# A hybrid decoder layer: in-projection tiles by Strassen's method first, and all heads' keys ahead of the delta rules

## The chip, the core and the metric

The kernel runs on one core of a Trainium2 chip. A core has TensorE (PE, matrix products into PSUM banks; PEld are its weight loads), VectorE (DVE), ScalarE (ACT), GpSimd (POOL) and SyncE (SP). Each works through a queue of its own in order; they wait for one another by semaphores. DMAs are issued here from SP's and POOL's queues. The metric is device time of one execution in microseconds (us), the median of several runs; lower is better.

## The reference

One layer of a decoder, over 512 prompt tokens and 8 sample tokens (520 columns, NTOK), in float32:

```python
xn   = rmsnorm(h, norm_mix)                         # 2048 wide
proj = xn @ w_in                                    # 2048 -> 5136: q | k | v | z | beta, decay | pool
q,k,v = silu(short_conv(proj[q,k,v], conv_w))       # causal, 4 taps; 8 heads of 128 each
q,k  = l2norm(q) * 128**-0.5, l2norm(k)
o    = gated_delta_chunked(q, k, v, g, beta)        # prompt; sample tokens: one recurrent step
dn   = rmsnorm(o, dn_norm) * silu(z)
pool = multiscale_pool(proj[pool])                  # 4 groups, trailing means of 2, 4, 8, 16
h    = h + concat(dn, pool) @ w_out
h    = h + (silu(gate) * up) @ w_down               # SwiGLU, d_ff = 5632
y    = rmsnorm(h, norm_final)
```

The delta rule of a head needs, for each block of tokens, the inverse of a unit lower triangular matrix 1 + M with M = strict(beta k k' decay).

## The kernel before, in words

Every float32 operand is cut into two fp32r halves: `hi`, a cast on ACT, and `lo`, the rest, by a subtraction on DVE. A product takes three passes, hi·hi, hi·lo and lo·hi. Activations lie transposed: `xh`, `xl` are the halves of the normed x as 16 tiles of 128 x 520 (token columns). A weight tile of 128 columns comes by SP as two `raw` loads of 512 KB, each cut once.

`product()` makes one 128-column tile of the projection: 16 k x 3 passes x 2 chunks of columns (264 and 256) = 96 matmuls into two banks named `mm`. The second chunk follows the first by SKEW = 3 k's. When a chunk is done, an eviction (`normed_out`, L259, DVE) scales it out of its bank. After each k, `weave.step()` lets other work, written as generators that yield, put its instructions into the queues; `weave.add(gen, queue, n)` starts one after n such steps. One product is 16 steps. So what stands between the matmuls of a product on PE is set by these counts.

A Strassen pair (`Pair`, `strassen()`; the out-projection, gate/up and down stages use them already) makes two 128-column tiles at once from half matrices: 7 products of 8 k x 3 passes with 260 columns, 168 matmuls into banks named `dn` in place of 192. It needs sums of weight blocks (DVE, `add`), sums of the activations' quarters (the forms T1 to T4) and sums of the results (`combine`, `out`).

The in-projection's order before: the transposes of x and the tiles k0, k1 in a first phase; then, for b in 0, 1 (four heads each): four k tiles, with `keys(h)` woven under them 16 steps apart; `eliminate(b)`; four z tiles; four times the q and the v tile of a head and, woven under the next, its `delta(h)`. Behind come the sample tokens' rules, woven under 8 pool tiles.

- `qkv_tile` evicts a tile to `ext` and applies the convolution on DVE (L739, L741: four operations of 128x512) and SiLU on ACT.
- `keys(h)` needs kT: it makes k k' and k's transpose on PE, norms, then `nn` (L783 on DVE, in mixb, one slot for each head of four) and `kd`. The four 32 x 32 diagonal blocks of nn go to DRAM (`nd_d`, four SP DMAs) and are then zeroed by four POOL memsets, which wait for those DMAs.
- `eliminate(b)` loads the diagonal blocks of four heads as `nb`, 64 partitions, and inverts them by 31 pairs of dependent DVE operations (L809 tm, L811 u). u and its transposed copy `ut` (L814) go to DRAM (`ud_d`); `qv_tiles` reads a head's blocks back as `utf`, four DMAs.
- `delta(h)` begins on PE with nn x utf (L833), then solves between blocks and runs the recurrence over four chunks.

Of the kernel before, what the change touches and what calls it, by code (L numbers as in the profile page):

```python
# [69 lines left out]
def decoder_kernel(ctx, tc, x_prompt, x_sample, state_delta, state_conv, state_pool, norm_mix, w_in,  # L70
# [94 lines left out]
    def step(acc, w, hi, lo, ci, k):  # L165
        c0, c1 = CHUNKS[ci]
        wh, wl = w[k]
        te.matmul(acc[ci], wh, hi[k][:, c0:c1], start=(k == 0), stop=False)  # L168
        te.matmul(acc[ci], wh, lo[k][:, c0:c1], start=False, stop=False)  # L169
        te.matmul(acc[ci], wl, hi[k][:, c0:c1], start=False, stop=(k == len(w) - 1))  # L170

    def product(w, hi, lo, evict, skew=SKEW):
# [8 lines left out]
        for i in range(K + skew):  # L181
            if i < K:
                step(acc, w, hi, lo, 0, i)
                if i == K - 1:
                    finish(0)
            if i >= skew:
                step(acc, w, hi, lo, 1, i - skew)
                if i < K + skew - 1:
                    weave.step()
# [71 lines left out]
    def columns():  # L261
        ext = pre.tile([P, 3 + SEQ], F32, tag="ext", name="ext", bufs=2)
        pool.memset(ext[:, 0:3], 0.0)
        return ext

    def to_columns(ext, t, ci, acc):
        if ci == 0:
            normed_out(ext[:, 3:3 + 256], acc, NB, 264, 0)
            normed_out(ccs[:, :, t], acc, 0, NB, 0)
        else:  # L270
            normed_out(ext[:, 3 + 256:3 + 512], acc, 264, NTOK, 264)

    with tc.tile_pool(name="ph0", bufs=2) as ph0, tc.high_priority(offset=10 * AHEAD), tc.manual_schedule():
        pr0 = ph0.tile([KT, P], F32, name="pr0", bufs=1)
        pr1 = ph0.tile([112, P], F32, name="pr1", bufs=1)
        pr2 = ph0.tile([32, P], F32, name="pr2", bufs=1)  # L280
        wba_raw = ph0.tile([P, KT, 16], F32, name="wba_raw", bufs=1)
        ss0 = ph0.tile([P, 10], F32, name="ss0", bufs=1)
        rs0 = ph0.tile([P, 8], F32, name="rs0", bufs=1)
        sel = ph0.tile([P, NB], F32, name="sel", bufs=1)
        xts = [ph0.tile([P, D if ti else P], F32, name=f"xt{ti}", bufs=1) for ti in range(5)]

        def span(ti):
            return slice(NB + P * (ti - 1), NB + P * ti) if ti else slice(0, NB)

        def square_sums(ti, eng, cols=slice(0, D), j=0):  # L290

            src, out = xts[ti][:, cols], ss0[:, 2 * ti + j:2 * ti + j + 1]
            sq = ph0.tile([P, D // 2], mybir.dt.bfloat16, name=f"sq{j}", bufs=1)[:, :src.shape[1]]
            if eng is act:
                act.activation(sq, src, AF.Square, accum_out=out)
            else:
                dve.scalar_tensor_tensor(sq, src, 1.0, src, op0=ALU.mult, op1=ALU.mult, accum_out=out)

        def roots(ti):
            s, r = ss0[:, 2 * ti:2 * ti + 1], rs0[:, ti:ti + 1]  # L300
            dve.tensor_tensor(s, s, ss0[:, 2 * ti + 1:2 * ti + 2], op=ALU.add)
            dve.tensor_scalar(s, s, 1.0 / D, EPS, op0=ALU.mult, op1=ALU.add)
            pow_mhalf(r, s)

        def diagonal(ti):
            dg = ph0.tile([P, P], F32, name="dg")
            dve.tensor_scalar(dg, ident, rs0[:, ti:ti + 1], None, op0=ALU.mult)
            return dg

        def spread(dg):  # L310
            pb = pst()
# [100 lines left out]
        for i in range(4):  # L412
            B[i].turn((0,))

# [1664 lines left out]
```

## Time and profile before

| | us |
|---|---|
| median of three runs | 2162.64 (2162.12 to 2162.88) |
| profiled execution | 2162.58 |
| its span | 2160.9 |
| PE busy in it | 2134.7 |
| DVE busy | 1746.6 |
| ACT busy | 928.6 |
| mean granted clock of TensorE | 0.999 |

The profile is of one execution; the span goes from its first instruction to its last. Busy time counts an instruction from start to end, and matmuls overlap, so that the spacing of their starts, not their duration, tells what one costs. A row of a group reads: line, engine, operation, output<-input, sizes, x count, busy us, mean ns, and the idle time before with what ended it. A row of the timeline reads: start, duration, engine (SPq is SP's queue of DMAs), line, operation, and in brackets the idle time before it and its releaser.

### The profile page before, as it was taken

To read this page: it belongs to the slowest core of one execution; us is meant where nothing else is said; L and a number is where in the kernel's file an instruction comes from. 1 tells how busy PE (TensorE), PEld (TensorE's weight loads), DVE (VectorE), ACT (ScalarE), POOL (GpSimd) and SP (SyncE) were. 2 spreads that over 40 slices of the span, in tenths; PEclk is the share of its full clock that TensorE was granted. 3 is DMA by queue.
4 is the path that set the end of the run, shared out by engine and by line. 5 is a ranking of instruction groups with operands and counts; after the bars stand their busy time and mean duration, and the time that the engine had idled before them with its cause. 6 is when DMAs were issued, how large, how long until landed. Compare 5 with 4: busy or idle time off the path is not lost.

```text
span 2160.9 us, 42982 instructions
## 1 busy us (share of the span) xinstructions
PE 2134.7 (99%) x17809; PEld 2127.9 (98%) x17809; DVE 1746.6 (81%) x2620; ACT 928.6 (43%) x1402; POOL 432.9 (20%) x512
## 2 busy tenths in 40 slices
PE   7999999999999999999999999999999999999998
PEld 7999999999999999999999999999999999999998
DVE  7686667666499979988888888988877898887997
ACT  5533443433264545434434434434434444435444
POOL 2210110101012212233233233232113302003100
PEclk9999999999999999999999999999999999999999
DMA  8343234323445443554554554554456746438333
GB/s 271 93 115 88 78 97 111 89 76 87 124 126 161 147 124 108 157 162 142 148 163 137 151 165 141 146 162 137 122 147 187 235 111 205 115 103 251 89 108 119
DMA packets 442498, 297.06 MB, mean 137 GB/s; under 512 B 26556, under 2 KB 423253, under 8 KB 438957
## 3 DMA queue, kind: packets, MB, share of 16 engines
q1 hardware_dynamic: 422877, 220.01, 36.2%
q0 software_dynamic: 18256, 73.55, 10.7%
q8 instruction: 140, 2.29, 0.5%
q10 hardware_dynamic: 1168, 0.74, 0.1%
q14 instruction: 57, 0.47, 0.1%
HBM read 251.47 MB, written 43.43 MB: 136 GB/s over the span
## 4 chain that ended last, share of the span: by engine, by line
PE 88%; DVE 7%; ACT 2%; issue 1%; DMA 1%; POOL 1%; SPq 0%; DVEq 0%; ACTq 0%; POOLq 0%
PE dn L1225 21%; PE dn L1224 21%; PE dn L1226 21%; PE mm L168 6%; PE mm L170 6%; PE mm L169 6%; DVE lo L1218 1%; PE dn L852 1%; DVE lo L137 1%; DMA st<-a_d 1%; DVE raw L1246 0%; POOL st L1778 0%; PE dn L962 0%; PE dn L859 0%; DVE tm L809 0%
## 5 line engine op out<-in xcount | busy, mean ns | idle before, releaser
L1217 ACT CAST hi<-raw 128x1024 fp32r<-128x1024 f32 (+1 forms) x422 | 427.5, 1027 | 404.2 <-DVE raw L1246 202.1
L1218 DVE TENSOR_TENSOR lo<-raw,hi 128x1024 fp32r<-128x1024 f32 (+1 forms) x422 | 529.2, 1275 | 88.0 <-ACT hi L1217 86.1
L168 PE MATMUL mm<-xh,hi 128*128 128x256 f32 (+1 forms) x1280 | 379.6, 297 | 2.6 <-DVE mixa L259 2.6
L170 PE MATMUL mm<-xh,lo 128*128 128x256 f32 (+1 forms) x1280 | 361.8, 283 | 1.5 <-DVE lo L137 1.5
L169 PE MATMUL mm<-xl,hi 128*128 128x256 f32 (+1 forms) x1280 | 361.4, 282 | 1.3 <-DVE xl L350 1.1
L168 PEld LDWEIGHTS mm<-xh,hi 128*128 128x128 f32 x1280 | 241.4, 189 | 3.7 <-DVE mixa L259 3.2
L169 PEld LDWEIGHTS mm<-xl,hi 128*128 128x128 f32 x1280 | 241.7, 189 | 1.9 <-DVE xl L350 1.9
L170 PEld LDWEIGHTS mm<-xh,lo 128*128 128x128 f32 x1280 | 240.8, 188 | 1.7 <-DVE lo L137 1.7
L1225 PE MATMUL dn<-b21l,hi 128*128 128x260 f32 x620 | 175.7, 283 | 0.3 <-DVE b21l L1788 0.3
L1226 PE MATMUL dn<-b21h,lo 128*128 128x260 f32 x620 | 175.4, 283 | 0.0
L1246 DVE TENSOR_TENSOR raw<-raw 128x1024 f32<-128x1024 f32 (+1 forms) x130 | 173.5, 1335 | 2.2
L1224 PE MATMUL dn<-b21h,hi 128*128 128x260 f32 x620 | 174.9, 282 | 0.0
L1226 PE MATMUL dn<-b11h,lo 128*128 128x260 f32 x612 | 173.2, 283 | 1.2 <-DVE lo L1218 1.2
L1225 PE MATMUL dn<-b11l,hi 128*128 128x260 f32 x612 | 173.3, 283 | 0.0
L1224 PE MATMUL dn<-b11h,hi 128*128 128x260 f32 x612 | 172.7, 282 | 0.0
L1224 PE MATMUL dn<-T1h,hi 128*128 128x260 f32 x556 | 158.1, 284 | 0.0
L1225 PE MATMUL dn<-T1l,hi 128*128 128x260 f32 x556 | 157.7, 284 | 0.0
L1226 PE MATMUL dn<-T1h,lo 128*128 128x260 f32 x556 | 156.7, 282 | 0.0
L1224 PE MATMUL dn<-B22h,hi 128*128 128x260 f32 x548 | 155.9, 284 | 0.0
L1225 PE MATMUL dn<-B22l,hi 128*128 128x260 f32 x548 | 155.6, 284 | 0.0
L1226 PE MATMUL dn<-B22h,lo 128*128 128x260 f32 x548 | 154.6, 282 | 0.4 <-DVE lo L1218 0.4
L135 ACT CAST hi<-raw 128x1024 fp32r<-128x1024 f32 (+2 forms) x86 | 87.1, 1014 | 150.5 <-PE mm L169 146.2
(659 smaller groups left out, 6420.8 us busy)
## 6 DMA issues: line engine op xcount, KB each, us to landing
raw<-in_w_gate_up_dram SPq DMA_DIRECT2D x134, 512.0 KB
raw<-in_w_in_dram SPq DMA_DIRECT2D x79, 512.0 KB
a_d<-mixa POOLq DMA_DIRECT2D x22, 1040.0 KB, 5.5
raw<-in_w_down_dram SPq DMA_DIRECT2D x48, 448.0 KB
mixb<-in_w_gate_up_dram SPq DMA_DIRECT2D x41, 512.0 KB
raw<-in_w_out_dram SPq DMA_DIRECT2D x25, 512.0 KB
st<-a_d POOLq DMA_DIRECT2D x49, 260.0 KB, 6.4
raw<-in_w_down_dram SPq DMA_DIRECT2D x24, 512.0 KB
```

The lines of the kernel that those rows point to most:

```text
L135: act.copy(hi[:, r], raw[:, r])
L137: dve.tensor_tensor(lo[:, r], raw[:, r], hi[:, r].bitcast(F32), op=ALU.subtract)
L168: te.matmul(acc[ci], wh, hi[k][:, c0:c1], start=(k == 0), stop=False)
L169: te.matmul(acc[ci], wh, lo[k][:, c0:c1], start=False, stop=False)
L170: te.matmul(acc[ci], wl, hi[k][:, c0:c1], start=False, stop=(k == len(w) - 1))
L852: te.matmul(yp[0:96, c, j], xt_[:, c, :], udf[:, c, j] if it == 0 else v3(cur)[:, c, j], start=True, stop=True)
L1217: act.copy(hi, raw)
L1218: dve.tensor_tensor(lo, raw, hi.bitcast(F32), op=ALU.subtract)
L1224: te.matmul(acc, wh[:, k, :], xf[:, k, :], start=start and k == 0, stop=False)
L1225: te.matmul(acc, wh[:, k, :], xg[:, k, :], start=False, stop=False)
L1226: te.matmul(acc, wl[:, k, :], xf[:, k, :], start=False, stop=stop and k == wh.shape[1] - 1)
L1246: dve.tensor_tensor(r[name], r[a], r[b], op=op)
```

## The change

- The in-projection begins with five pairs of tiles, k2 to k7 and z0 to z3: (k2, k3) and (k4, k5) as plain pairs in the same half matrices (192 matmuls of 260 columns), while ACT and DVE make the forms from x in mixa and mixb, then (k6, k7), (z0, z1), (z2, z3) by Strassen. T1 takes the place of a quarter of xh, xl; at the last pair that quarter is made again from x in DRAM (`xs_d`), under the next product, which therefore begins with its second eight k's.
- Every q, k, v tile is evicted whole and goes through DRAM (`c_d`, a POOL DMA); `convolved()` reads it back and does convolution and SiLU when it is wanted.
- `keys(h)` of all eight heads follow one another, five steps between nn and the next part, under q and v products. Heads 4 to 7 keep kT in mixa[4..6], nn in mixa[7] alone and kd in one buffer, and store all three to DRAM (`kept_d`); `come_back(h)` fetches them when head h-4 is done.
- One `eliminate()` works on all heads, 128 partitions. It reads back utf of heads 0 and 1 and adds `delta(0)`, 60 steps later; each delta adds the next.
- The products that follow: q0, v0, q1, v1, ... q6, v6, z4, z5, q7, v7, z6, z7, then the pool tiles.

The helpers of the Strassen pairs move up in the text unchanged and are left out here, as is the making of the forms.

```diff
+    class InPair(Pair):
+        def __init__(self, t0):
+            self.out_tiles = {}
+            super().__init__(lambda i, j: win_view(in_cols(t0 + i))[:, 8 * j:8 * j + 8, :], self.to)
+            self.t0 = t0
+        def to(self, i, half, a, b):
...
+            dve.tensor_tensor(o[:, c], a, b, op=ALU.add)
+            dve.tensor_tensor(o[:, c], o[:, c], rb[:, c], op=ALU.mult)
+            if t >= 24:
+                act.activation(o[:, c], o[:, c], AF.Silu)
+            elif not first:
+                stored(o, t)
...
+        plain_pairs = InPair(10), InPair(12)
+        pairs = [InPair(14), InPair(24), InPair(26)]
...
+        plain_pairs[0].plain(to_plain)
+        plain_pairs[1].plain(to_strassen)
...
+            if j == 0:
+                pool.dma_start(b12, xs_d[0:8].rearrange("k p c -> p k c")[:, :, HALF:])
...
+                for k in range(8):
+                    act.activation(hi[:, k, :], b12[:, k, :], AF.Copy, scale=nmix(k))
+                for k in range(8):
+                    dve.scalar_tensor_tensor(lo[:, k, :], b12[:, k, :], nmix(k), hi[:, k, :].bitcast(F32),
+                                             op0=ALU.mult, op1=ALU.subtract)
+        strassen(pairs, fb[:, 0:HG * P], after, xap)
...
+    def stored(o, t):
+        pool.tensor_copy(ccs[:, :, t], o[:, 0:NB])
+        pool.tensor_copy(ccp[:, :, t], o[:, NTOK - 3:NTOK])
+        pool.dma_start(c_d[t], o[:, NB:NTOK])
...
+        def convolved(x, t):
+            pool.memset(x[:, 0:3], 0.0)
+            sp.dma_start(x[:, 3:3 + SEQ], c_d[t])
+            y = d1tile("y", [P, SEQ], "y")
...
+        def places(h):
+            a, b = (mixb[:, h, :], mixb[:, 4 + h, :]) if h < 4 else (mixa[:, 4 + (h - 4) % 3, :], mixa[:, 7, :])
+            return a[:, NB - 3:NTOK], b[:, 0:SEQ]
+        def come_back(h):
+            kd = kds[h] = d1tile("kd", [P, SEQ], "kd")
+            for i, x in enumerate((mixb[:, h % 4, NB:NTOK], mixb[:, 4 + h % 4, 0:SEQ], kd)):
+                sp.dma_start(x, kept_d[h - 4, i])
...
         def keys(h):
-            kT, nn = mixb[:, h % 4, 0:SEQ], mixb[:, 4 + h % 4, 0:SEQ]
-            kd = kds[h] = d1tile("kd", [P, SEQ], "kd")
+            x, nn = places(h)
+            kT = x[:, 3:3 + SEQ]
+            kd = kds[h] = d1tile("kd" if h < 4 else "qts", [P, SEQ], "kd")
+            if h + 2 < H:
+                take_k(h + 2)
...
-            yield 6 if h < 3 else 2
+            yield 5
...
+            if h >= 4:
+                for i, y in enumerate((kT, nn, kd)):
+                    sp.dma_start(kept_d[h - 4, i], y)
+            if h == H - 1:
+                weave.add(eliminate(), 1)
...
-        def eliminate(b):
-            nb = d1tile("nb", [64, 32, 32], "nb")
+        def eliminate():
+            nb = d1tile("nb", [P, 32, 32], "nb")
...
+            for h in range(2):
+                load_u(h)
+            take_qv(0)
+            weave.add(delta(0), 0, 60)
             yield 1
...
-        for b in range(2):
-            for h in range(4 * b, 4 * b + 4):
-                qkv_tile(1, h, mixb[:, h % 4, 0:SEQ],
-                         {0: ext_first, 1: ext_second}.get(h))
...
-                weave.add(keys(h), 1, 16)
-            weave.add(eliminate(b), 1)
-            for h in range(4 * b, 4 * b + 4):
-                z_tile(h)
-            for h in range(4 * b, 4 * b + 4):
-                qv_tiles(h)
+        for h in range(2):
+            take_k(h)
+        weave.add(states())
+        weave.add(gates(), 1)
+        for h in range(H):
+            weave.add(keys(h), 1)
+        for h in range(H):
+            qkv_tile(h, None if h else w_next)
+            qkv_tile(16 + h)
+            for z in {6: (4, 5), 7: (6, 7)}.get(h, ()):
+                z_tile(z)
```

What this does to the queues shows at three places.

DVE, the end of the elimination. Before, in `eliminate(0)` (tm is the product with a column of nb, u the running inverse, ut its transposed copy, lo a weight cut, ext an evicted tile):

```order
L809 TENSOR_TENSOR tm<-nb,u 64x87
L811 TENSOR_TENSOR u<-u,tm 64x3x29
L809 TENSOR_TENSOR tm<-nb,u 64x60
L811 TENSOR_TENSOR u<-u,tm 64x2x30
L809 TENSOR_TENSOR tm<-nb,u 64x31
L811 TENSOR_TENSOR u<-u,tm 64x31
L814 COPY ut<-u 64x1024
L137 TENSOR_TENSOR lo<-raw,hi 128x1024
L259 TENSOR_TENSOR ext<-mm,rb 128x256
```

After:

```order
L261 TENSOR_TENSOR ext<-mm,rb 128x264
L1202 TENSOR_TENSOR u<-u,tm 128x6x26
L1200 TENSOR_TENSOR tm<-nb,u 128x135
L1202 TENSOR_TENSOR u<-u,tm 128x5x27
L1200 TENSOR_TENSOR tm<-nb,u 128x112
L1202 TENSOR_TENSOR u<-u,tm 128x4x28
L1200 TENSOR_TENSOR tm<-nb,u 128x87
L1202 TENSOR_TENSOR u<-u,tm 128x3x29
L1200 TENSOR_TENSOR tm<-nb,u 128x60
L1202 TENSOR_TENSOR u<-u,tm 128x2x30
L1200 TENSOR_TENSOR tm<-nb,u 128x31
L1202 TENSOR_TENSOR u<-u,tm 128x31
```

The eviction of a product's first chunk now stands ahead of the last eleven steps; the rows that follow are the copy ut (L1205), then work of delta(0).

PE, the beginning of `delta(0)`. Before:

```order
L168 MATMUL mm<-xh,hi 128x256
L169 MATMUL mm<-xl,hi 128x256
L170 MATMUL mm<-xh,lo 128x256
L833 MATMUL dn<-utf_644,mixb 128x96 x4
L840 MATMUL dn<-ident,qT 128x128 x4
L168 MATMUL mm<-xh,hi 128x264
```

After, beginning with the last three matmuls of the first chunk (264 columns) whose eviction heads the DVE rows above:

```order
L170 MATMUL mm<-xh,hi 128x264
L171 MATMUL mm<-xl,hi 128x264
L172 MATMUL mm<-xh,lo 128x264
L170 MATMUL mm<-xh,hi 128x256
L171 MATMUL mm<-xl,hi 128x256
L172 MATMUL mm<-xh,lo 128x256
L1234 MATMUL dn<-utf_1937,mixb 128x96 x4
L1241 MATMUL dn<-ident,qT 128x128 x4
```

The first use of utf stands three matmuls behind that chunk's last; before, the products of four z tiles, q0 and v0 lay between the elimination's beginning and it.

SP, from the diagonal blocks to utf. Before:

```order
L799 DMA nb<-nd_d 64x1024
L131 DMA raw<-in_w_in_dram 128x8x128 x5
L812 DMA ud_d<-u 16x4x1024
L815 DMA ud_d<-ut 16x4x1024
L131 DMA raw<-in_w_in_dram 128x8x128
L1095 DMA utf_644<-ud_d 32x8x32 x3
```

After:

```order
L1132 DMA gcb<-gcr_d 128x512
L1190 DMA nb<-nd_d 128x1024
L1183 DMA kept_d<-mixa 128x512
L131 DMA raw<-in_w_in_dram 128x8x128 x5
L1203 DMA ud_d<-u 32x4x1024
L1206 DMA ud_d<-ut 32x4x1024
L1127 DMA utf_1937<-ud_d 32x8x32 x4
```

The stores of u are twice as large, a kept_d store (mixa is kT or nn) has come in behind nb, and no weight load stands between the stores and the read-backs.

1734 lines of the change are left out of this document (921 added, 813 removed).

## The prediction

> **What bounds the kernel now.** I read the page's engine lines first, then busy time by stretch, then what PE waits for.
>
> ```profile
> span 2160.9 us, 42982 instructions
> PE 2134.7 (99%) x17809; PEld 2127.9 (98%) x17809; DVE 1746.6 (81%) x2620; ACT 928.6 (43%) x1402; POOL 432.9 (20%) x512
> PE 88%; DVE 7%; ACT 2%; issue 1%; DMA 1%; POOL 1%; SPq 0%; DVEq 0%; ACTq 0%; POOLq 0%
> 108.00:162.00 54.00, 51.44 (x424) 50.82 (x424) 44.81 (x112) 16.93 (x22) 5.64 (x15) 1.00 0.44 115
> 162.00:594.00 432.00, 432.00 (x3711) 431.90 (x3710) 275.31 (x637) 161.96 (x344) 40.70 (x96) 1.00 0.35 94
> 1080.00:2160.00 1080.00, 1073.15 (x8920) 1072.70 (x8919) 910.88 (x1122) 463.27 (x603) 242.29 (x238) 1.00 0.51 150
> PE mm L168 <- DVE mixa L259: 2.6, 3, 1.2
> ```
>
> The engine lines, the chain that ended last (88% PE) and the stretches (start:end, length, then busy time of PE, PEld, DVE, ACT, POOL) say the same: TensorE is the bound, all the way. From 162 to 594 us, the in-projection's main part, it idles for nothing at all; so a matmul less there is its whole spacing less, and a wait newly put into PE's queue there is paid in full, since nothing follows that PE could run instead. One stretch of the in-projection, 108 to 162, lacks 2.56 us; the last row (waits of PE: total, times, longest) names it: PE waited three times for evictions on DVE. This is where `eliminate(0)` runs on DVE between them.
>
> **The change, part by part.**
>
> *Matmuls.* Ten of the projection's tiles (k0 to k7 less the two of the first phase, z0 to z3) are made otherwise: 960 matmuls of 264 or 256 columns become two plain pairs (2 x 192) and three Strassen pairs (3 x 168), 888 matmuls of 260. A single matmul's duration overlaps the next, so I take the spacing of starts:
>
> ```profile
> 140.68 0.28 PE L169 MATMUL mm<-xl,hi 128*128 128x256 f32 x1
> 151.84 0.28 PE L169 MATMUL mm<-xl,hi 128*128 128x264 f32 x1
> 1479.78 0.28 PE L1226 MATMUL dn<-B22h,lo 128*128 128x260 f32 x1
> 1503.39 0.28 PE L1224 MATMUL dn<-b11h,hi 128*128 128x260 f32 x1
> ```
>
> The first two are 93 matmuls apart (0.1200 us each), the last two 196 (0.1205). 960 x 0.1200 = 115.2 us goes, 888 x 0.1205 = 107.0 comes: **-8.2 us**. Forms and sums for Strassen are made on DVE and ACT from data on chip; the same scheme runs in the gate/up stage at 911 of 1080 us of DVE and 6.9 us of PE idle in 1080, so for a stretch of 107 us I count 0 and keep 4 for the upper end. Filling and storing c_d (24 DMAs of 256 KB, 48 short copies on POOL, which is 20% busy) and reading it back is hidden by PE's products while the reads come well ahead; 0. Restoring the overwritten part of xh/xl at the last pair (8 ACT, 8 DVE operations of 260 columns, some 0.4 us each) lies under that pair's last 24 matmuls and the first eight k of the next product, 48 more, 8.7 us in all: 0; without that cover the next product would start 3 us late.
>
> *The old eliminate.* Its evictions' waits, the 2.6 us above, go with their place: **-2.6**. The single new one on 128 partitions has the same 62 dependent steps of the same length, for a step's time goes with its columns. That saves DVE one pass of 28 us, from which PE gains nothing, since it waited for nothing else there (432.00 of 432.00 beside the second pass).
>
> *All keys in a row.* Heads 4 to 7 put nn into one buffer, mixa[7]. Before the next head's nn can be written, four nd_d stores, four memsets on POOL and a kept_d store of 256 KB must end. DVE waits in order at the next nn, with evictions behind it.
>
> ```profile
> 111.77 1.12 DVE L783 SCALAR_TENSOR_TENSOR mixb<-dn,sck,dm 128x128 f32<-128x128 f32 x4
> 109.10 5.54 SPq L790 DMA_DIRECT2D nd_d<-mixb  x8
> 114.41 0.19 POOL L793 MEMSET mixb<- 32x128 f32 x1 [2.21 <-DMA nd_d<-mixb]
> 115.80 0.20 POOL L793 MEMSET mixb<- 32x128 f32 x1 [0.29 <-DMA nd_d<-mixb]
> out_dram<-ub POOLq DMA_DIRECT2D x16, 256.0 KB, 3.1
> st<-a_d POOLq DMA_DIRECT2D x49, 260.0 KB, 6.4
> ```
>
> nn takes 1.1 us on DVE; from its end (112.8) to the last memset's (116.0) pass 3.2; the store has no row in before, and lies between 3.1 (a store of 256 KB) and 6.4 (a read of about that on a busy queue), nearer the first, being a store too. So about 7.4 us a head against a spacing on PE of five steps of a sixteenth product (0.72 us) and its own small matmuls, about 5 us (an estimate: 3.6 and some 1.4). Three heads wait in this way, at most 3 x 2.4 = 7 us. An eviction may be late by some 24 matmuls, 2.9 us, before PE needs its bank, and each wait is 2.4: nearly all is absorbed, what adds up is not. I take **+2.5**, bounds 0 and 7.
>
> *The eliminate that delta(0) stands behind.* It is now alone, and its u must go through DRAM before delta(0)'s first matmul (L1234), which in PE's queue is a fixed 60 weave steps after it. Before, four z tiles, q0 and v0, six products, lay between. In the changed order the eviction L261 of the product under way stands on DVE ahead of the last eleven elimination steps. That eviction can't begin before the last first-chunk matmul of that product; and L1234 stands only three matmuls behind that one on PE. So this tail is paid by PE whatever came earlier; DVE, SP and the DMA go through it in series:
>
> ```profile
> 145.46 0.31 DVE L811 TENSOR_TENSOR u<-u,tm 64x156 f32<-64x156 f32 x1
> 148.33 0.19 DVE L811 TENSOR_TENSOR u<-u,tm 64x31 f32<-64x31 f32 x1
> 148.55 1.11 DVE L814 COPY ut<-u 64x1024 f32<-64x1024 f32 x1
> 127.83 0.41 DVE L259 TENSOR_TENSOR mixa<-mm,rb 128x264 f32<-128x264 f32 x1
> 128.17 0.37 DVE L811 TENSOR_TENSOR u<-u,tm 64x220 f32<-64x220 f32 x1
> 148.59 0.61 SPq L812 DMA_DIRECT2D ud_d<-u  x1
> 149.69 0.55 SPq L815 DMA_DIRECT2D ud_d<-ut  x1
> 152.83 2.40 SPq L1095 DMA_DIRECT2D utf<-ud_d  x3
> 155.77 2.56 SPq L1095 DMA_DIRECT2D utf<-ud_d  x5
> 160.03 0.61 POOL L837 COPY uu<-utf 128x512 f32<-128x512 f32 x1 [3.60 <-DMA utf<-ud_d]
> ```
>
> Step by step: the matmul itself 0.3; the eviction 0.34 (127.83 to 128.17); from the 156-column step to the transposing copy 3.09 (145.46 to 148.55); to ud_d<-ut 1.14 (149.69); to the first read-back 3.14 (152.83), which waited for both stores. These are twice as large now (128 partitions). Of the 3.14, 0.55 is the issue; if the other 2.6 went with the bytes it would be 2.6 more, if none did, 0; I take 1.1, nearer the fixed end. L1234 needs three read-backs: 2.4 us to issue as before, and the last issue of before (158.33) landed 1.7 before 160.03; but in before a weight load lay among them, so 3.5 for both, at least 2.8 and at most the 7.2 that all eight took. Sum 0.3 + 0.34 + 3.09 + 1.14 + 4.24 + 3.5 = 12.6; PE works for 0.5 of it: **+12.1**, bounds 10.3 and 17.3. What is late next is DVE's work behind the copy (L1255, evictions), which waits for PE itself.
>
> A page of the Trainium skill prices the stores otherwise: "DMA: Bandwidth & Descriptors", section "Anatomy of one DMA", gives 2.0 us fixed and the bytes at 436 GB/s, so an estimate of 3.2 us for 512 KB from its issue, where I have 4.24. By it the sum would be 1.0 less; the trace's 3.14 for 256 KB is above that page's 2.6.
>
> *The delta rules.* The reads of c_d, kept_d and utf join SP's queue ahead of weight loads, some 12 issues of 0.5 us (2.56 for five, above) a head against two products of 11.5 us, 23 us; z4 to z7, q and v are the same products in another order. 0. Out-projection and FFN are as they were; the helpers only move in the text.
>
> *Sum* against the profiled execution, 2162.58 us (span 2160.9, 1.7 around it, 0.06 under the median of 2162.64): 2162.6 - 8.2 - 2.6 + 2.5 + 12.1 = **2166.4**, 0.17% above before. The kernel gives its gain back at one place.
>
> **The rivals.** A (the forecast): the tail of eliminate costs 10 to 14 us, the keys 0 to 5: 2162 to 2169.5.
>
> B, faster: the tail is short. For it: the steps of before were interleaved with two weight loads, and a load stood among their read-backs, which leaves something to save. Against: the steps, copy and the two stores alone are 0.3 + 0.34 + 3.09 + 1.14 + 3.14 - 0.5 = 7.5 before the first read-back. It decides below 6.5 us of tail with nothing lost at the keys (2162.6 - 10.8 + 6.5 = 2158.3); at 5 us, 2157. That needs half the measured rows, or a queue order on the chip that lets the steps run before the eviction.
>
> C, much slower: the keys' single buffer. For it: kept_d's stores share SP's queue with nd_d and weight loads, each store waits for its data there, and the 6.4 us row. At 6.4 a head takes 10.7, three heads 17 us late, of which slack takes 3 x 2.9: +8.4, so 2172.3 beside A's tail.
>
> D, the Strassen pairs don't pay in this place: DVE, at 80 to 95% of the stretch by my count of its operations, makes PE wait.
>
> ```profile
> L1218 DVE TENSOR_TENSOR lo<-raw,hi 128x1024 fp32r<-128x1024 f32 x338 | 439.7, 1322 | 78.3 <-ACT hi L1217 77.2 <-DMA out_dram<-st 0.2
> L137 DVE TENSOR_TENSOR lo<-raw,hi 128x1024 fp32r<-128x1024 f32 x80 | 97.7, 1222 | 54.5 <-ACT hi L135 54.3
> ```
>
> The same cut takes 1222 ns in the in-projection and 1322 beside the FFN's work on POOL. Some forty such operations stand in the stretch; 4 us more on DVE, and as much on PE if it has no slack: with it 2170.4. Were all 8.2 us eaten, 2174.6. Against: in the FFN DVE is as full and PE idles 0.6%. On this the Trainium skill, "SBUF — State Buffer", section "Who interferes with whom", says that a DVE instruction with two SBUF inputs blocks, or is blocked by, a GpSimd one that reads SBUF. The two rows agree; by it the change's POOL copies would speak for D, but they are short.
>
> **How the numbers follow.** 0.2% of 2162.64 is 4.3 us, about what a measurement of this kernel can tell from no change: below 2158.3 is faster, above 2167.0 slower. A has 0.72, and its 2162 to 2169.5 straddles the upper bound: 0.43 same, 0.28 slower, 0.01 faster. B 0.12, C 0.10, D 0.06; C and D are slower. B is faster for 0.10, same for 0.02. Sums: faster 0.11, same 0.45, slower 0.44. The predicted time is A's. For 8 in 10 the range runs from the lower end of A less 2 (a shorter read-back with the 10.3) to C: 2160 to 2172.5. A's own is 2162 to 2169.5.
>
> **What would show it.** In the profile after: matmuls of 260 at about 0.1205 us between 48 and 160 us with PE full there, or D. On PE's waits, one row L1234 <- DMA utf<-ud_d, of 10 to 14 us, some 50 us behind the last key's matmuls, with eleven L1200/L1202 steps, L1205, two ud_d stores and three read-backs in series before it: A; under 6, B. PE waits for L261, with DVE waiting for kept_d or POOL's memsets at L1170, sum to 0 to 5: A; 8 and more: C. Wrong altogether would be a stretch that I cost at 0: deltas waiting for kept_d or c_d, or the pool and sample stage, which now begins 1.3 us and ends 7.8 us sooner in PE's count.

## The result, and the profile after

The changed kernel takes 2196.5 us (2194.5 to 2198.0), the one before 2162.5 on the same chip (2162.1 to 2162.9): a ratio of 1.0157, 95% interval 1.0139 to 1.0174, 34 us slower. That is 24 us above the upper end of the predicted range. First the page: span, engines, and the chain that ended last.

```profile
span 2196.3 us, 43075 instructions
PE 2139.0 (97%) x17737; PEld 2127.6 (97%) x17737; DVE 1786.2 (81%) x2635; ACT 958.0 (44%) x1454; POOL 455.7 (21%) x559
PE 77%; DVE 11%; DMA 4%; ACT 3%; issue 3%; POOL 1%; SPq 0%; ACTq 0%; DVEq 0%; POOLq 0%
```

The 72 matmuls are gone (17809 to 17737), yet PE's share of the chain fell from 88 to 77%; DVE, ACT, DMA and "issue" took it. The same three stretches as before (columns as there, the last three the granted clock, the DMA share and GB/s):

```profile
108.00:162.00 54.00, 52.54 (x435) 51.81 (x435) 43.70 (x63) 24.31 (x36) 6.94 (x11) 1.00 0.50 142
162.00:594.00 432.00, 400.00 (x3345) 394.65 (x3344) 290.32 (x705) 178.10 (x393) 67.09 (x156) 0.97 0.44 124
1080.00:2160.00 1080.00, 1079.89 (x8968) 1079.57 (x8968) 922.05 (x1118) 462.60 (x597) 247.05 (x239) 1.00 0.52 151
```

The loss lies in the middle row. Where PE had been busy for 432.00 of 432.00 us with 3711 matmuls, it is busy for 400.00 with 3345, at a clock of 0.97. 366 matmuls less, at the 0.1164 us that one took there before, are 42.6 us, about the loss and the gain that it swallowed. Under the Strassen pairs, 97.0 to 154.6, PE is busy throughout (what 108 to 162 lacks, 1.46 us, is the first product behind them waiting for its weight's two halves), and so it is in the FFN. What PE waited for (total, times, longest), and one row of DVE's waits:

```profile
PE dn L1234 <- DMA utf<-ud_d: 13.6, 1, 13.6
PE dn L1282 <- DVE S L1297: 8.6, 6, 2.0
PE dn L1155 <- ACT mixa L1100: 4.3, 1, 4.3
PE mm L1549 <- DVE xl L197: 2.9, 4, 1.2
PE dn L1158 <- DVE mixb L1170: 2.8, 1, 2.8
```

```profile
DVE y L1097 <- DMA vT<-c_d: 10.3, 7, 3.5
```

These five rows of PE sum to 32.2 us. Only the first was in the forecast's sum at such a size. They don't make up the loss: the changed kernel also saves 8 on matmuls and no longer pays the 2.6 at L168, so some 44 us are to be found. The rest is smaller waits and a slow clock, below.

To place the loss I use PE's *lateness*: the start of a stage's first matmul in the trace, less all that stands ahead of it in PE's program at the spacings of a busy PE. It grows only where PE waits or runs slowly. The whole program is 2117.7 us long in this count before and 2110.0 after, 7.7 shorter (the forecast's spacings make it 8.2). What a stage adds to the lateness is called its loss.

| lateness, us | first key | key 7 | delta 0 | delta 1 | sample stage | out-projection |
|---|---|---|---|---|---|---|
| before | 18.6 | 22.4 | 22.0 | 22.1 | 23.1 | 30.8 |
| after | 19.9 | 28.0 | 44.4 | 50.6 | 62.9 | 70.9 |

(Before, keys 4 to 7 come after delta 3.) After loses 8.1 in the keys, 16.4 from the last key to delta 0 (13.6 at L1234, the rest mostly the slow clock behind the wait at the last key), 6.2 in delta 0, 12.3 in deltas 1 to 7; the sample stage adds 7.7 before and 8.0 after, nearly alike, mostly because the count takes its matmuls of two columns too short. 40.1 more lateness less 7.7 of program is 32.4; another 2.9 is the L1549 row at the out-projection's start, and that makes the span's 35.4.

**The tail.** The timeline ahead of delta 0, DVE, SP and PE:

```profile
293.42 0.29 PE L172 MATMUL mm<-xh,lo 128*128 128x264 f32 x1
294.06 1.22 DVE L137 TENSOR_TENSOR lo<-raw,hi 128x1024 fp32r<-128x1024 f32 x1
296.18 0.42 DVE L261 TENSOR_TENSOR ext<-mm,rb 128x264 f32<-128x264 f32 x1
296.52 0.31 DVE L1202 TENSOR_TENSOR u<-u,tm 128x156 f32<-128x156 f32 x1
299.68 1.03 DVE L1205 COPY ut<-u 128x1024 f32<-128x1024 f32 x1
299.67 0.64 SPq L1203 DMA_DIRECT2D ud_d<-u  x1
300.74 0.54 SPq L1206 DMA_DIRECT2D ud_d<-ut  x1
304.75 5.32 SPq L1127 DMA_DIRECT2D utf<-ud_d  x9
307.70 1.99 PE L1234 MATMUL dn<-utf,mixb 128*128 128x96 f32 x8 [13.63 <-DMA utf<-ud_d]
```

Eviction to step 0.34, step to copy 3.16, copy to the second store's issue 1.06, to the first read-back 4.01, to L1234 2.95: 11.5 together. The forecast had 0.34, 3.09, 1.14, 4.24 and 3.5, which is 12.3. The other 2.1 of the 13.6 lie ahead of the eviction: its chunk's last matmul (first row) ends at 293.7 and PE stops at 294.1, but DVE has a weight cut (second row) and three elimination steps to do before it. The forecast let the eviction follow the matmul at once.

**The clock behind it.** The same place in slices of 2 us, and two of 3.41 us behind it; the third column from the end is the granted clock:

```profile
298.00:300.00 2.00, 0.00 (x0) 0.00 (x0) 1.76 (x8) 0.00 (x0) 0.00 (x0) 0.75 0.21 64
308.00:310.00 2.00, 2.00 (x11) 2.00 (x11) 0.00 (x0) 0.27 (x1) 0.61 (x1) 0.50 0.34 52
310.00:312.00 2.00, 2.00 (x12) 2.00 (x11) 0.00 (x0) 1.47 (x8) 0.61 (x1) 0.50 0.11 16
312.00:314.00 2.00, 2.00 (x18) 2.00 (x18) 1.09 (x5) 0.20 (x2) 1.10 (x2) 0.84 0.05 12
314.00:316.00 2.00, 2.00 (x20) 2.00 (x19) 1.88 (x5) 1.05 (x1) 0.82 (x3) 1.00 0.32 34
322.88:326.29 3.41, 1.63 (x14) 1.43 (x13) 3.24 (x7) 2.68 (x3) 0.00 (x0) 1.00 0.00 2
326.29:329.70 3.41, 3.41 (x18) 3.41 (x18) 2.17 (x3) 0.55 (x2) 0.00 (x0) 0.50 0.30 77
```

PE's last matmul before the wait ends at 294.1. The clock falls to 0.50 at about 299 and is back at about 312.6, 4.9 us after the first new matmul; in those, matmuls of 256 columns start 0.21 us apart in place of 0.12. So the wait of 13.6 costs 4.9 x (1 - 0.12/0.21) = 2.1 us more, which no row of waits shows. The wait of 4.3 us at 236 does the same: 11 matmuls in each of the two slices of 2 us from 237 to 241, 18 in the next. And it falls once more, from 326.3 to 329.7 (last row), though the only wait before is the 1.78 us for S at 325.3, shown below; at the spacings of 0.21 and 0.12 that is another 1.5 us.

**The last key.** SP, DVE and PE:

```profile
226.85 0.53 SPq L1095 DMA_DIRECT2D mixa<-c_d  x1
231.15 0.49 DVE L1097 TENSOR_SCALAR y<-mixa,prm 128x512 f32<-128x512 f32 x1
234.61 0.75 DVE L1099 SCALAR_TENSOR_TENSOR y<-mixa,prm,y 128x512 f32<-128x512 f32 x1
236.07 2.08 PE L1155 MATMUL dn<-mixa 128*128 128x128 f32 x8 [4.35 <-ACT mixa L1100]
```

Head 7's kT takes mixa[4], head 4's place, so its read from c_d can't be early: in SP's queue it comes behind head 4's store of kd to kept_d (225.23) and a weight load. Its four convolution steps then come among evictions and cuts on a full DVE and take from 231.15 to 235.4.

**The delta rules.** PE, SP, DVE and PE again, in delta 0:

```profile
316.50 0.60 PE L1268 MATMUL dn<-ident,vT 128*128 128x128 f32 x4
317.14 0.48 SPq L1095 DMA_DIRECT2D vT<-c_d  x1
322.98 0.49 DVE L1097 TENSOR_SCALAR y<-vT,prm 128x512 f32<-128x512 f32 x1 [3.48 <-DMA vT<-c_d]
324.96 0.28 DVE L1297 COPY S<-dn 128x128 f32<-128x128 f32 x1
325.30 0.49 PE L1282 MATMUL dn<-S,mixb 128*128 128x128 f32 x2 [1.78 <-DVE S L1297]
```

`take_qv(h+1)` is called in the middle of delta h. v has a single place, which PE frees by the transposes at 316.50; only then can the next v be read, and the first convolution step stands on DVE, waiting for the data until 322.98. The state S of the recurrence stands behind it in DVE's queue though its product had ended on PE at 322.6, and PE stands behind S. DVE waited so 7 times, 10.3 us in all.

### The profile page after: what moved, and what is told of

It is laid out like the page before. It is cut to its first block, busy times and chain, and to the rows that moved or that the text cites. A ratio compares the mean times of both kernels' runs of the same rounds, so it can differ in the third digit from the quotient of the medians.

```text
span 2196.3 us, 43075 instructions
## 1 busy us (share of the span) xinstructions
PE 2139.0 (97%) x17737; PEld 2127.6 (97%) x17737; DVE 1786.2 (81%) x2635; ACT 958.0 (44%) x1454; POOL 455.7 (21%) x559
## 4 chain that ended last, share of the span: by engine, by line
PE 77%; DVE 11%; DMA 4%; ACT 3%; issue 3%; POOL 1%; SPq 0%; ACTq 0%; DVEq 0%; POOLq 0%
PE dn L301 21%; PE dn L302 21%; PE dn L303 21%; PE mm L170 3%; PE mm L172 3%; PE mm L171 3%; DVE lo L295 2%; DVE lo L137 1%; DMA vT<-c_d 1%; DVE y L1099 1%; ACT hi L294 1%; DVE raw L323 1%; DMA st<-a_d 1%; DMA raw<-in_w_in_dram 0%; DVE tm L1200 0%
## 5 line engine op out<-in xcount | busy, mean ns | idle before, releaser
L294 ACT CAST hi<-raw 128x1024 fp32r<-128x1024 f32 (+1 forms) x447 | 453.1, 1027 | 439.1 <-DVE raw L323 218.2
L295 DVE TENSOR_TENSOR lo<-raw,hi 128x1024 fp32r<-128x1024 f32 (+1 forms) x447 | 556.8, 1265 | 104.4 <-ACT hi L294 102.8
L170 PE MATMUL mm<-xh,hi 128*128 128x264 f32 (+1 forms) x960 | 291.1, 303 | 1.4 <-DVE ext L261 0.7
L171 PE MATMUL mm<-xl,hi 128*128 128x264 f32 (+1 forms) x960 | 272.5, 284 | 1.3 <-DVE xl L586 1.1
L172 PE MATMUL mm<-xh,lo 128*128 128x264 f32 (+1 forms) x960 | 272.6, 284 | 1.1 <-DVE lo L137 1.1
L170 PEld LDWEIGHTS mm<-xh,hi 128*128 128x128 f32 x960 | 182.7, 190 | 2.4 <-DVE ext L261 0.9
L171 PEld LDWEIGHTS mm<-xl,hi 128*128 128x128 f32 x960 | 183.0, 191 | 1.9 <-DVE xl L586 1.9
L172 PEld LDWEIGHTS mm<-xh,lo 128*128 128x128 f32 x960 | 181.9, 189 | 1.6 <-DVE lo L137 1.6
L323 DVE TENSOR_TENSOR raw<-raw 128x1024 f32<-128x1024 f32 (+1 forms) x136 | 180.5, 1327 | 2.3
L303 PE MATMUL dn<-B22h,lo 128*128 128x260 f32 x548 | 154.6, 282 | 0.4 <-DVE lo L295 0.4
L1605 POOL TENSOR_TENSOR mixa<-mixa 128x520 f32<-128x520 f32 x22 | 51.2, 2326 | 495.7 <-DVE mixa L1599 495.7
```

Source lines behind the costliest of these rows:

```text
L170: te.matmul(acc[ci], wh, hi[k][:, c0:c1], start=(i == 0), stop=False)
L172: te.matmul(acc[ci], wl, hi[k][:, c0:c1], start=False, stop=(i == len(w) - 1))
L294: act.copy(hi, raw)
L295: dve.tensor_tensor(lo, raw, hi.bitcast(F32), op=ALU.subtract)
L303: te.matmul(acc, wl[:, k, :], xf[:, k, :], start=False, stop=stop and k == wh.shape[1] - 1)
L323: dve.tensor_tensor(r[name], r[a], r[b], op=op)
```

## The experiments

My theory after this reading: three causes, each a chain through DRAM put where PE's program has nothing else to run (the tail, the last key's place, v's place), and behind long waits the clock. Rivals: that DVE has too much work beside the keys and deltas whatever the places (then reads and places change nothing), that Strassen doesn't pay here, and that the tail alone pulled everything behind it along. Each kernel is the changed one with the edit shown, timed beside the kernel before.

**Delta 0 later.** It starts 80 weave steps after the eliminate in place of 60; the sample products give up half their steps to make room.

```diff
-            weave.add(delta(0), 0, 60)
+            weave.add(delta(0), 0, 80)
```

> delta(0) is started 80 steps after the elimination in place of 60 (14.4 us of products more between them), and the later sample products give up some of their spacing so that the sample tokens still end before the out-projection. Theory 1 (the loss sits at three separate places: 13.6 us wait for utf with the slow clock behind it, some 8 us at the keys, 9 to 14 us at the delta rules' first S): only the first goes, L1234's wait falls from 13.6 to under 1 us and TensorE isn't slow behind it, 16 to 19 us in all, so 2178 to 2181. Rival (DVE is short as a whole, and the wait only shows where PE meets it): the wait turns up at another line and the time stays above 2190.

2193.2 us (2187.3 to 2199.3), ratio 1.0142 (1.0117 to 1.0168); profiled span 2190.1.

```profile
PE dn L1234 <- DMA utf<-ud_d: 4.3, 1, 4.3
PE dn L1376 <- DMA s<-in_state_delta_dram: 2.5, 2, 1.3
PE dn L1282 <- DVE S L1297: 1.3, 3, 1.0
594.00:648.00 54.00, 50.91 (x357) 49.80 (x357) 30.71 (x70) 17.68 (x31) 1.23 (x4) 0.84 0.32 92
```

The tail's wait is 9.3 shorter and the waits for S nearly go. But the sample stage, denser and begun later, now waits for its states from DRAM, at a clock of 0.84 in its stretch: the lateness at its start is 47.6 (62.9 in after), at its end 64.5 (70.9). The time is hardly told from after's: what was saved is lost two stages on. So the expected 2178 to 2181 is missed, and what the rival named came true. One more thing is to be seen here: v's place is untouched, yet DVE waits only 2.2 us for v (10.3 in after) and PE 1.3 for S. The two waits go together, and how long they are hangs on when delta 0 begins. The deltas still lose some 12.5 (18.5 in after).

**The reads of q and v early.** Those of head h+1 are issued at the start of delta h, v alternately in two places.

```diff
+            if h + 1 < H and 17 + h in traced:
+                fetch_qv(h + 1)          # q in s0; v in ("s2", "u")[h % 2]
```

> The c_d reads of the next head's q and v are issued at the start of delta(h), v into two places in turn (tag s2 and u), while the convolution stays where it is. Theory 1 (DVE waits at the next head's v for a read that was issued only after PE had done with the one place of v, and the copy of S stands behind it on DVE): L1282's waits for S, 8.6 us, fall to 1 to 3, and the time falls by 7 to 12 us to 2185 to 2190. Rival (the eight convolution operations themselves, 5.3 us a head, hold up S, whenever the reads land): under 3 us of change, 2194 to 2197. The wait at L1234 stays 13 to 14 us by both.

2194.7 us (2190.7 to 2195.1), ratio 1.0142 (1.0127 to 1.0158).

```profile
PE dn L1252 <- DMA utf<-ud_d: 13.6, 1, 13.6
PE dn L1300 <- DVE S L1315: 2.6, 4, 1.0
```

The waits for S fall from 8.6 to 2.6, so the read of v caused most of them. The loss from delta 0 to the sample stage falls only from 18.5 to 12.9: 2.4 of waits for W on ACT are new, and delta 0 still runs into the slow clock after the 13.6. The time moved by less than the runs scatter: the waits came out as the theory had them, the time as the rival had it.

**Places of their own.** nn of heads 5 and 6, kT of head 7 and kd of every second head go to other buffers.

```diff
-            a, b = ... (mixa[:, 4 + (h - 4) % 3, :], mixa[:, 7, :])
+                placed[h] = (mixa[:, h, :] if h < 7 else d1tile("aq", [P, NTOK], "kT7"),
+                             mixa[:, 7, :] if h in (4, 7) else d1tile("uu", [P, SEQ], "nn"))
```

> Keys of heads 4 to 7 get more places: nn of heads 5 and 6 in the two uu buffers, kT of head 7 in aq, kd in qts and vs in turn, so that no key waits for the kept_d stores of the one before. Theory 1 (the reused places make the last key late, PE then idles 4.3 us at L1155 and runs slow behind it): that wait goes, with 2 us of slow clock, and the time falls by 5 to 8 us, 2188 to 2191. Rival (DVE is saturated by the keys in a row, with 2.8 us at L1158 as its sign): the waits move to other lines of the same stretch and less than 2 us is gained. The wait at L1234 stays as it is by both, since its chain starts at an eviction.

2186.1 us (2184.4 to 2186.9), ratio 1.0106 (1.0091 to 1.0121): the largest single step, 10.4.

```profile
PE dn L1242 <- DMA utf<-ud_d: 6.5, 1, 6.5
PE dn L1166 <- DVE mixb L1178: 3.0, 1, 3.0
```

The 4.3 at the last key is gone; the loss in the keys falls from 8.1 to 5.0. So the 10.4 are in part luck, for the tail's wait halved too, which the edit doesn't touch: the order on DVE came out otherwise, with the eliminate's copy (289.11) ahead of the next eviction of 264 columns (291.26). That is the queue order of the prediction's rival B. The tail's price hangs on which eviction falls into the last steps. The edit moves nn, kT and kd at once, so it doesn't tell which of these places counted.

**Filling the wait.** 104 matmuls of 260 into an unused bank ahead of delta 0's first one.

```diff
+            if h == 0:
+                for i in range(104):
+                    te.matmul(junk_[:, :HALF], xh[:, i % KT, 0:P], xh[:, i % KT, 0:HALF], ...)
```

> 104 matmuls of 260 columns, 12.5 us, whose result nobody reads, stand in PE's queue ahead of delta(0)'s first matmul, in the time in which PE otherwise waits for utf. Theory 1 (TensorE's clock falls in a long wait and costs some 3 us after it, here 307.7 to 313.6 with matmuls 0.21 us apart in place of 0.12): the granted clock stays at 1.00 there and the time falls by 2 to 5 us, to 2192 to 2195, though PE does 12.5 us more work. Rival (the slow matmuls are hidden behind delta(0)'s own dependent chain): no change, 2196 to 2197; if the fill were not covered by the wait, 2200 and more.

2197.4 us (2195.1 to 2199.8), ratio 1.0159 (1.0144 to 1.0174): no change.

```profile
PE dn L1286 <- DVE S L1301: 10.4, 6, 3.3
PE dn L1238 <- DMA utf<-ud_d: 1.2, 1, 1.2
270.00:324.00 54.00, 50.46 (x425) 49.87 (x424) 36.28 (x92) 11.40 (x21) 5.42 (x14) 1.00 0.41 119
```

With PE kept busy the clock there is 1.00 (0.87 in after) and delta 0 loses 2.4 in place of 6.2. So about 3.8 us of delta 0's loss is the slow clock (2.1 and 1.5 above). But the deltas behind lost it again at S (10.4, longest 3.3, with a clock of 0.94 in one later stretch). The slow clock is real and no term that can simply be added.

**All three, then with room.** Early reads, places, delta 0 at 70 steps (first label). Then, besides, half steps for the sample products of heads 4 to 7 and a third place for their states (second label).

```diff
-                    yield 1
+                    if j % 2 or h < 4:
+                        yield 1
-            s0 = d1tile("uu", [P, 4, P], "s0")
+            s0 = d1tile(("uu", "uu", "y")[(2 * h + hf) % 3], [P, 4, P], "s0")
```

> The three cures together: more places for the keys of heads 4 to 7, the c_d reads of q and v issued a delta ahead, and delta(0) 70 steps behind the elimination (with the places, its wait had fallen to 6.5 us at 60, and 10 steps are 7.2 us). Theory 1 (three separate places, whose costs add): against 2196.5, the places bring 10 (measured), the last 6.5 us of wait with the slow clock behind it 8, the early reads 4 to 6: 2172 to 2176. What is left then is 3 us at L1158 in the keys, some 8 us in the delta rules, and before is still 10 us faster. Rival (DVE is short as a whole): what is taken away at one place comes back at the next, 2183 to 2187 as with the places alone.

> The three cures of e5 with room at the end: the sample products of heads 4 to 7 take half as many weave steps, and their states load into three places (uu, uu, y) in place of two, so that the sample tokens end 16 us of PE work before the out-projection in place of 2. Theory 1: e5 waited 6.4 us at the out-projection's start for x's cut, since the sample tokens' end had moved onto it, and 1.4 us for states; both go: 2179.3 less 6 to 9, 2170 to 2173. Rival (the sample products then wait for their loads at twice the pace, as they did in e1): the wait moves to L1376's states and nothing is gained, 2178 to 2182.

2179.3 us (2178.5 to 2182.0), ratio 1.0084 (1.0067 to 1.0101); and **2169.5** (2167.7 to 2171.3), ratio 1.0032 (1.0019 to 1.0044). The first one's new row, then two of the second:

```profile
PE mm L1574 <- ACT xh L196: 6.4, 1, 6.4
```

```profile
162.00:594.00 432.00, 420.56 (x3576) 415.41 (x3574) 299.33 (x727) 181.48 (x401) 70.58 (x160) 1.00 0.47 132
PE dn L1182 <- DVE mixb L1194: 3.7, 2, 2.7
```

| lateness, us | first key | key 7 | delta 0 | delta 1 | sample stage | out-projection |
|---|---|---|---|---|---|---|
| all three | 19.9 | 25.7 | 30.4 | 31.0 | 36.8 | 52.7 |
| with room | 19.6 | 24.3 | 29.1 | 29.8 | 35.7 | 43.9 |

With all three, delta 0's loss is that of before (0.6; 0.1 there) and PE has its full clock. Deltas later by ten steps pushed the sample stage's end against the out-projection, which waited 6.4 us for its cut input, so that the expected 2172 to 2176 was missed by 3; that is what "room" takes back. 27 of the 34 us are recovered without a change to what is computed. That is strong evidence for the theory: every engine has the same work as in after, only places and times moved. How the 27 divide isn't shown: alone, delta 0 later (80 steps), early reads and places brought 3.3, 1.8 and 10.4. Nor is there a kernel with delta 0 later and room but neither early reads nor places, so the rival that the tail pulled the rest along is weakened by the 12.5 above, not excluded.

**Two eliminations, keys under the deltas.** As before the change in outline: four heads each, keys 4 to 7 beside the first deltas, 16 steps apart, delta 0 at 80, early reads.

```diff
-            if h == H - 1:
-                weave.add(eliminate(), 1)
+            if h % 4 == 3:
+                weave.add(eliminate(h // 4), 1)
```

> One part of the change undone: two eliminations of four heads each as in before. The first follows the keys of heads 0 to 3, delta(0) comes 80 steps behind it (1.4 us of PE work earlier than in the changed kernel), and the keys of heads 4 to 7, 16 steps apart, and the second elimination run beside the first delta rules; q's and v's reads are issued earlier, into the same places. Theory 1 (keys and the one elimination crowded in front of the deltas, with a DRAM round trip as their end on the path, cost what the change lost): the waits at L1155 and L1234 go, 4.3 and 13.6 us and the slow clock behind both, and the time falls to 2168 to 2175. Rival (DVE is short as a whole from the keys to the last delta): the second elimination's 28 us on DVE beside the deltas holds up their dependent steps, waits at L1282 to L1299 grow, and it stays above 2180.

2187.0 us (2185.8 to 2188.9), ratio 1.0117 (1.0101 to 1.0132).

```profile
PE dn L1313 <- DVE S L1328: 9.5, 5, 3.5
PE mm L170 <- DVE ext L261: 4.8, 4, 2.0
```

The waits for utf and at the last key are gone (lateness 28.2 at delta 0), but from there to the sample stage it loses 24, as the rival, load on DVE beside the deltas, had it. The longest wait for S, 3.5, does stand behind elimination steps on DVE. But v has its single place in this kernel too, DVE waits for it six times, 6.8 us, and the other four waits for S each follow such a wait. So load is a part, and its share isn't shown.

**Wider spacing of the keys.** The last good kernel with six steps in a key (delta 0 at 68), then seven (and half sample steps from head 2).

> As h1, with six steps in place of five behind each key (5.8 us more products among the keys) and delta(0) 68 steps behind the elimination. Theory 1 (five steps a key are less than DVE's work for a key, and PE waits for banks that nn's writing frees, 5.5 us in e5 at L1182): these waits fall to under 3 us, at an equal time elsewhere: 2167 to 2171. Rival (they come from the order on DVE at one place, the first convolutions, not from its load): no change against h1.

> As h2 with seven steps behind each key, and half the sample steps from head 2 on. Theory 1: the waits at the keys all but vanish (under 1 us) and the time is 2165 to 2169; what stays against the 2154 to 2155 of the matmul count alone is the slow clock behind the remaining waits and the sample stage. Rival (load, not spacing): as h2 or, by the tighter sample products, slower.

2182.4 us (2180.8 to 2182.8; ratio 1.0089, 1.0074 to 1.0104) and 2192.3 us (2184.9 to 2199.0; 1.0136, 1.0102 to 1.0170). Both are misses. A row of each:

```profile
PE dn L1260 <- DMA utf<-ud_d: 6.4, 1, 6.4
```

```profile
PE mm L170 <- DVE ext L261: 8.6, 6, 2.2
```

More room for each key moved the eliminate against the evictions again: the tail's wait is back, or evictions wait behind its steps. One step more in a key, with delta 0 two steps earlier, costs 13 us. That the order on DVE is why is read from these rows, not tested.

**Strassen undone.** The kernel with room, its three Strassen pairs as plain pairs.

```diff
-        strassen(pairs, fb[:, 0:HG * P], after, xap)
+        pairs[0].plain(following(pairs[1], fb[:, 0:HG * P]))
+        pairs[1].plain(following(pairs[2], r21a))
+        pairs[2].plain(last)
```

> The kernel of h1_room with its three Strassen pairs made as plain pairs (72 matmuls of 260 columns more; forms and sums on DVE gone). Theory (the Strassen term is what the prediction took, 0.12 us a matmul, all of it on the path): 72 x 0.1205 = 8.7 us above h1_room's 2169.5, so 2176 to 2180. Rival D (Strassen's saving is eaten by DVE): less than 4 us above h1_room, 2169 to 2173.

2176.1 us (2175.9 to 2176.4), ratio 1.0065 (1.0050 to 1.0080): 6.6 above the kernel with room, the runs 4.6 to 8.6 apart. So the 72 matmuls are worth most of their 8.7 in this place, and the rival that Strassen doesn't pay here falls.

**What is left in the keys.** The kernel with room still loses 4.7 in the keys, nn late on DVE and PE's transposes behind the bank that it holds. Five kernels, each with one thing moved or left out: two taps of the keys' convolution; the first tap of every convolution from DVE to ACT; the convolution behind nn; one decay row for all keys; no power on POOL.

```diff
-                for i in range(1, 4):
+                for i in range(1, 2 if 8 <= t < 16 else 4):      # two taps
-            dve.tensor_scalar(y, x[:, 0:SEQ], cw(0, t), None, op0=ALU.mult)
+            act.activation(y, x[:, 0:SEQ], AF.Copy, scale=cw(0, t))   # tap on ACT
-            pow_mhalf(rr, ss)
+            dve.tensor_scalar(rr, ss, 0.0, 0.05, ...)            # no power
```

> The kernel of h1_room with the convolution of the keys left at two of its four taps (part of the computation left out: some 1.3 us of DVE less a head). Theory (DVE's load in the stretch of the keys makes PE wait there): the waits for mixb in the keys, some 5.7 us in h1_room, fall below 2 us, and the time to 2163 to 2167. Rival (not DVE's load but the order of waits, for nn's stores and kT's read): the waits stay at 4 to 6 us and the time at 2168 to 2171.

> The kernel of h1_room with the first tap of every convolution on ACT instead of DVE (24 passes of 512 columns, some 0.5 us each, moved). Theory (DVE's load beside keys and delta rules is what remains): the keys' and the delta rules' waits for DVE get shorter, 2165 to 2168.5. Rival (ACT's queue, behind evictions and state copies, delays the convolution as much as it relieves DVE): 2169 to 2174.

> The kernel of h1_room with the convolution of the head after next written behind nn and kd of the head in hand, not ahead of them. Theory (nn stands in DVE's queue behind the convolution and the decay rows, so the bank that it frees comes late): the waits L1182 <- DVE mixb/nn, 4.9 us in h1_room, fall below 2 us, the time to 2164 to 2167. Rival (the chain of squares, power and scales sets nn's time): the waits stay above 4, 2168 to 2172.

> The kernel of h1_room with the decay rows of head 0 used for the keys of all heads (part of the computation left out: seven reads of gcb of the keys and their 28 operations on DVE). Theory (dm waits on DVE for gcb, whose read stands on SP behind stores that wait for nn, and nn stands behind dm): waits for mixb and nn below 2 us, 2163 to 2167. Rival (gcb's wait is covered): above 4, 2168 to 2171.

> The kernel of h1_room with a constant in place of the power on POOL in the keys (part of the computation left out: the norm of the keys). Theory (the chain over POOL, 0.95 to 1.25 us of DVE's idle time a head, sets nn's time): waits below 3 us, 2165 to 2168. Rival (DVE's order, or gcb): 2168 to 2171.

| | us | ratio (95%) | loss in the keys, us |
|---|---|---|---|
| with room | 2169.5 (2167.7 to 2171.3) | 1.0032 (1.0019 to 1.0044) | 4.7 |
| two taps | 2169.1 (2168.4 to 2169.8) | 1.0033 (1.0020 to 1.0045) | 6.7 |
| tap on ACT | 2173.2 (2171.3 to 2174.8) | 1.0051 (1.0036 to 1.0066) | 10.7 |
| convolution behind nn | 2168.6 (2167.6 to 2169.7) | 1.0029 (1.0018 to 1.0040) | 5.1 |
| one decay row | 2167.0 (2164.8 to 2176.4) | 1.0029 (1.0017 to 1.0041) | 2.7 |
| no power | 2167.1 (2165.5 to 2168.0) | 1.0022 (1.0013 to 1.0032) | 4.1 |

The waits for nn's bank with two taps, with the tap on ACT, and with one decay row:

```profile
PE dn L1182 <- DVE mixb L1194: 4.4, 1, 4.4
```

```profile
PE dn L1182 <- DVE mixb L1194: 3.8, 2, 2.4
PE dn L1182 <- DVE mixa L1194: 2.6, 1, 2.6
```

```profile
PE dn L1187 <- DVE mixb L1199: 2.1, 1, 2.1
```

These losses hold the slow clock too, and it isn't alike: in the stretch of the keys it is at 0.50 for 6.8 us with two taps and with the tap on ACT, for 3.4 with the convolution behind nn, and never in the other three. So the five don't decide. With less work on DVE the waits at L1182 sum to 4.4 in place of 5.7, but come in one piece, and the clock falls behind it; DVE's load is neither shown nor excluded. With the convolution behind nn they are 5.1, with the tap on ACT 7.8. Without the reads of the decay rows, which stand on SP behind stores, the keys lose 2.0 less, without the power on POOL 0.6 less; the times are some 2.4 us lower, but their intervals overlap that of the kernel with room. What makes up the last 5 us of the keys stays open. No kernel that computes the whole reference beats the one before the change; the kernel with room, and with the convolution behind nn, come within about 0.3% of it.

## Why the prediction was wrong, point by point

- *Matmuls, -8.2*: right. 7.7 less by the count of PE's program, and 6.6 in the experiment for the 72 that Strassen saves. Rival D falls: PE is full under the pairs.
- *Old eliminate, -2.6*: right; no such row is left.
- *The tail, +12.1*: right in place and in the chain, the order of eleven steps behind the eviction included; the wait is 13.6. But that the sum came so near is in part luck: the five terms from the eviction on are 0.8 too long together, each within 0.6 of the trace, and the start is 2.3 too short, for DVE came to the eviction 2.1 after PE's stop where the sum has 0.3 less 0.5. So the tail is not paid "whatever came earlier": it is 6.5 where DVE is ahead (places of their own). On the stores, the Trainium skill's "DMA: Bandwidth & Descriptors", "Anatomy of one DMA", has a formula for DMAs that GpSimd issues, while these are SP's; by it the estimate is 3.2 where the forecast took 4.24. The trace has 4.01, nearer the forecast. What the term left out is the clock: 2.1 after this wait (counted in the deltas' 18.5 below).
- *Keys, +2.5 (0 to 7)*: 8.1, and by another wait. Only nn was looked at as a shared place, and nn's cost next to nothing: DVE waited 0.2 us for kept_d there. The place that PE waited for longest was kT's, mixa[4] for heads 4 and 7: read, convolution and SiLU in series, on a full DVE. And slack was counted for evictions, not for the five banks that gram and transposes share.
- *Delta rules, 0*: the step that failed. The span is 31.6 above the forecast's sum; 17.4 of that is here, 5.6 in the keys, 4.3 between the last key and delta 0, 2.9 at the out-projection. It counted 12 issues against 23 us of a head and asked whether SP's queue had time. It did not ask when v's read may start (when its single place is free, mid-delta) nor what stands behind the waiting convolution on DVE (S, for which PE waits). From delta 0 to the sample stage the loss is 18.5 us against 1.1 before. Early reads took 6.0 of the 8.6 us at S away, some 3.8 of the 18.5 are the slow clock in delta 0, and with the three edits together the stage loses 6.4; what the rest of the 18.5 is made of stays open. The prediction named this as what would make it wrong altogether, and put no price on it.
- *Out-projection, 0*: 2.9 at L1549, small.
- Rival C's 2172.3 had the sign and, in the keys, one of the stages right, with the wrong buffer and under a third of the loss.
- Forecast A's terms add up to 2161.8 to 2170.8, not to the 2162 to 2169.5 that it states; the measured time lies far above both.

## What to carry to other kernels

When a value that an engine held now comes back through DRAM, count more than the issues: from when its place is free until its data are there, and every instruction behind the first reader in that engine's queue. A place shared by two loop turns is a wait, and several such waits are priced only when all are taken away: here each edit alone was worth 2 to 10 us, together with room behind them 27. An experiment on one wait should be read at the end of the next two stages, for the gain may be lost there.

## What the runs showed of the hardware

A wait of 1.8 us can halve TensorE's granted clock, and one of 2.8 can leave it alone. In the changed kernel's trace the clock changes at 234.13 (to 0.50), 240.96 (to 1.00), 298.99, 312.64, 326.29 and 329.71 us. These times are 2, 17, 4, 4 and 1 times 3.413 us apart: all lie on one grid. The clock came back at the end of the first whole step of the grid in which PE worked, after the two long waits 4.9 us after the first matmul, with 0.21 us between matmuls until then. It fell at the end of a step in which PE was busy for 0.29, 0.00 and 0.48 of it; steps with 0.51 and 0.52 kept it. So the wait of 1.78 us that ends at 325.3, inside one step, cost the clock, and that of 2.83 us from 208.6 to 211.4, over two steps, did not. (In other kernels, in the sample stage or right behind it, the clock also fell at 0.56 to 0.90, so this is no exact rule.) The Trainium skill's "TensorE: Matmul & The Clock Gate", "What's actually happening", has a free-running window of about 3.4 us, of which one idle one halves the clock and one busy one opens it. The halving, the grid and the opening agree; the fall differs, for here a window only half idle was enough.

Some of these kernels scatter more from run to run: the one with seven steps in a key took 2184.9 us at a mean granted clock of 0.997 and 2199.0 at 0.989. That a wait falls now inside one step of the grid and now over two would explain it, but isn't shown.
